# Attention products with 128 rows and 128 columns of the array, and two heads transposed at once

## The chip, the cores and the metric

The kernel runs on one core of a Trainium2 chip. Its time is the device time in microseconds (us) of one execution. Three runs of the kernel before gave 2948.76, 2953.93 and 2954.27 us; the median is 2953.93.

## The reference

The input is one sequence of 512 tokens with 1024 features. A first block of two layers, then a second block of one layer, all in float32:

```python
for l in range(2):
    x = layer_norm(ALPHA * x + 0.5 * swiglu(x, ...))          # ffn1
    x = layer_norm(ALPHA * x + token_mixer(x, ...))           # latent + sparse attention
    x = layer_norm(ALPHA * x + 0.5 * swiglu(x, ...))          # ffn2
# second block: gated linear attention, convolution, differential attention, then experts
x = x + mix @ w_out
x = x + hier_moe(rms_norm(x), ...)
```

The token mixer has two attentions of eight heads each. Latent attention (`mla_attention`) is causal, with 64 + 32 features per query and key, and 64 per value. Sparse attention (`nsa_attention`) has 64 features, two groups of four heads that share keys and values, and three branches whose results are added under a gate: attention over 31 compressed blocks of keys (`compress`: windows of 32 tokens through a small network with a Gelu), over selected blocks, and over a window. With 512 tokens all eight blocks are selected and the window covers everything, so these two are causal attentions with keys and values of their own. Differential attention in the second block has four heads; each takes two causal softmax maps of 64 features and subtracts the second, times a factor, from the first.

## The kernel before

Float32 values are split in two halves of TensorE's faster float32 type: `hi` is the rounded value (ScalarE), `lo` the rest (VectorE, `split`, L205 and L206). A product of two such values is three products, hi x hi, lo x hi and hi x lo (`mm3`, L223 to L225); only lo x lo is left out.

**A unit** (`Unit`) is one head and one branch. It goes through four stages: `prep` (transposes the head's queries and keys so that features lie on the partitions, and splits them), `scores` for four blocks of 128 queries (`prob_block`: score products L499, the causal mask as a product with an identity L500, maximum L502, exponential L503, reciprocal L504, scaling by GpSimd L105), `turn` (`prob_T`: transposes of the probabilities, L516, and their split) and `values` (`products`: L124 and L127). `attend` runs units as a pipeline: in one step, unit n makes its scores, unit n-1 its transposes, unit n-2 its values; the preparation of unit n+2 stands at the end of the step. A first-block layer has 8 latent units and then 16 sparse ones (8 heads x 2 branches). Between the stages 16 chunks of a gate projection are woven in (`gate_chunk`, L223 to L225 with tile `g`), at 0.62 of a part per point. The order within each engine's queue is then fixed by the scheduler of the language when the program is built: it keeps the program's priority, and moves an instruction up where one before it is not ready by its own model.

**Rows and columns of the array.** A product's rows are its contraction, its columns the width of its weights. Latent scores have 96 features, three products with 96 rows. Sparse and differential scores stack the query: `q2` holds the hi half in partitions 0 to 63 and the lo half in 64 to 127, `kk` the key's hi half twice. One product with 128 rows gives (q hi + q lo) x k hi, a second one with 64 rows q hi x k lo (`kl`). In the values the weights are v hi and v lo side by side (128 columns), so that a product with the probabilities' hi half writes v hi x p hi to the upper and v lo x p hi to the lower 64 partitions of the output; the second product has only the 64 columns of v hi, with the probabilities' lo half. `put` adds the two output halves at the end.

**Preparation.** `head_q` and `head_k` handle one head: four transposes of 128 tokens x 64 features (L836, L824), then ScalarE writes the hi half (L838, L841; for keys twice, L825 and L826) and VectorE the lo half (L839, L842, L827). Sparse keys are prepared when a group's first head begins (heads 0 and 4), for both branches; queries once per head. Differential attention calls both for each of the two maps of a head (L1342, L1343).

**The compressed branch.** When the second head of a pair is prepared, `compressed` computes the scores of both heads against 32 compressed keys: for four blocks of tokens and two heads a product with 128 rows (L912) and one with 64 (L913), each 32 wide; then mask, softmax and gate on VectorE and ScalarE, four transposes (L930), and a split into two tiles. `nsa_end` adds this branch to the head's output with two products that have 32 rows (L762, L763), against `vcb`, the compressed values that `compress` made beside the query projection.

**Banks.** Score products, key and query transposes and gate chunks share four PSUM banks (`pa`), the transposes of probabilities and the outputs four others (`pb`).

Of the kernel before, what the change touches and what calls it, by code (L numbers as in the profile page):

```python
# [87 lines left out]
class Unit:  # L88
# [31 lines left out]
    def products(self, j, out, start, stop):  # L120

        mm, v = self.b.nc.tensor.matmul, self.v(j)
        ph, pl = self.b.keys_T(j, self.pT)
        both = lambda: mm(out[:, j * 128:], v, ph, start=start and j == 0, stop=stop and j == NT - 1)  # L124
        if j == 0:
            both()
        mm(out[:64, j * 128:], v[:, :64], pl, start=False, stop=False)  # L127
        if j > 0:
            both()


class DiffUnit(Unit):
# [28 lines left out]
class Build:  # L161
# [381 lines left out]
    def mixer_(self, es, l):  # L543
# [10 lines left out]
        ksw = [p1.tile([128, NT, 2, 64], F32, name=f"k{b}") for b in "sw"]  # L554
        vsw = [p1.tile([128, NT, 2, 64], F32, name=f"v{b}") for b in "sw"]
        gn = p1.tile([128, NT, 24], F32, name="gn")
        vcb = p1.tile([64, 2, 2, 64], F32R, name="vcb")
        kcd = [[p1.tile([128, 32], F32R, name=f"kcd{g}{j}") for j in range(2)] for g in range(2)]
        pro = ExitStack()
        p2 = pro.enter_context(tc.tile_pool(name=f"p2{l}", bufs=1, reuse_waits="tile"))  # L560
# [166 lines left out]
        def nsa_begin():  # L727
            big = [pm.tile([128, 3072], F32R, name=f"big{j}", tag=("q96", "k96")[j]) for j in range(2)]
            st["on"] = [x[:, :2048].rearrange("p (c n) -> p c n", c=4) for x in big]
            st["vn"] = [x[:, 2048:].rearrange("p (t g k d) -> p t g k d", t=NT, g=2, k=2) for x in big]  # L730
            st["pc"] = [self.base.tile([128, 2, 512], F32R, name="pc", tag=t) for t in ("gB", "bB")]
            for br in range(2):
                self.split(st["vn"][br][:, :, :, 0], st["vn"][br][:, :, :, 1], vsw[br])

        def nsa_prep(h, br):
            g = h // 4

            def prep():
                if h == 0 and br == 0:
                    nsa_begin()  # L740
                if h % 4 == 0 and br == 0:
                    kk = self.wh.tile([128, 1024], F32R, name="kk", tag="hi").rearrange("p (k n) -> p k n", k=2)
                    kl = self.wl.tile([128, 1024], F32R, name="kl", tag="lo").rearrange("p (k n) -> p k n", k=2)
                    for b in range(2):
                        self.head_k(kk[:, b], kl[:, b], lambda t: ksw[b][:, t, g, :])
                    st["k", g] = kk, kl
                kk, kl = st["k", g]
                if br == 0:
                    st["q", h % 2] = self.head_q(qn, h)
                q2 = st["q", h % 2]  # L750
                if h % 2 == 1 and br == 0:
                    self.compressed(h - 1, st["q", 0], st["q", 1], kcd[g], gn, cmask, valid,
                                    [x[:64, (h // 2) % 2] for x in st["pc"]])
                return (q2, q2[:64]), (kk[:, br], kl[:64, br])
            return prep

        def nsa_end(h):
            g, r = h // 4, slice((h % 2) * 32, (h % 2) * 32 + 32)

            def end(po):  # L760
                pc = [x[r, (h // 2) % 2] for x in st["pc"]]
# [57 lines left out]
    def head_k(self, kk, kl, src):  # L819

        nc = self.nc
        ps = self.pa()
        for t in range(NT):
            nc.tensor.transpose(ps[:64, t * 128:t * 128 + 128], src(t), self.ident)  # L824
        nc.scalar.activation(kk[:64], ps[:64], AF.Copy)  # L825
        nc.scalar.activation(kk[64:], ps[:64], AF.Copy)  # L826
        nc.vector.tensor_tensor(kl[:64], ps[:64], kk[:64].bitcast(F32), ALU.subtract)  # L827

    def head_q(self, qn, h, q2=None, g=None):

        nc = self.nc
        if q2 is None:
            q2 = self.wh.tile([128, 1024], F32R, name="q2", tag="hi")[:, :T]
        ps = self.pa()
        for t in range(NT):
            nc.tensor.transpose(ps[:64, t * 128:t * 128 + 128], qn[:, t, h, :], self.ident)  # L836
        if g is None:
            nc.scalar.activation(q2[:64], ps[:64], AF.Copy)  # L838
            nc.vector.tensor_tensor(q2[64:], ps[:64], q2[:64].bitcast(F32), ALU.subtract)  # L839
        else:  # L840
            nc.scalar.activation(q2[:64], ps[:64], AF.Copy, scale=g)  # L841
            nc.vector.scalar_tensor_tensor(q2[64:], ps[:64], g, q2[:64].bitcast(F32), op0=ALU.mult, op1=ALU.subtract)  # L842
        return q2

    def windows(self, kc_tm, vc_tm, blks):

# [17 lines left out]
    def compress(self, l, p2, blks, kcd, vcb):  # L864

        nc, a, par = self.nc, self.a, self.par
        w2 = p2.tile([128, 2, 128], F32, name="w2")
        nc.scalar.dma_start(w2, a["cw2"][l])
        for j in range(2):
            for g in range(2):  # L870
                nc.gpsimd.memset(kcd[g][j].bitcast(F32), 0.0)  # L871
        for kv in range(2):
            blk = blks[:, 2 * kv:2 * kv + 2].rearrange("p c t -> p (c t)")[:, :992].rearrange(
                "p (m n) -> p m n", m=16)
            ph = self.pa()[:, :62]
            for m in range(16):
                if m % 8 == 0:
                    w1 = self.wr.tile([128, 1024], F32, name="w1", tag="raw").rearrange("p (c h) -> p c h", c=8)
                    nc.sync.dma_start(w1, a["cw1"][l, kv, m // 8])
                nc.tensor.matmul(ph, w1[:, m % 8, :], blk[:, m],  # L880
                                 start=m == 0, stop=m == 15)
                yield
            b1 = par[:, (P_B1K, P_B1V)[kv]:(P_B1K, P_B1V)[kv] + 1]
            if kv == 0:
                hid = self.tmp.tile([128, 512], F32, name="hid", tag="tmp")[:, :62]
                nc.scalar.activation(hid, ph, AF.Gelu_apprx_tanh, bias=b1)
                pk = self.pa()[:, :62]
                nc.tensor.matmul(pk, w2[:, 0, :], hid, start=True, stop=True)
                for g in range(2):
                    hi, lo = kcd[g][0][:, :31], kcd[g][1][:64, :31]  # L890
                    nc.scalar.activation(hi, pk[:, g * 31:g * 31 + 31], AF.Copy)
                    nc.vector.tensor_tensor(lo, pk[:64, g * 31:g * 31 + 31], hi[:64].bitcast(F32), ALU.subtract)
            else:
                hid = self.tmp.tile([128, 512], F32, name="hid", tag="tmp")[:, :128]
                h4 = hid.rearrange("p (g r c) -> p g r c", g=2, r=2)
                nc.vector.memset(hid, 0.0)
                for g in range(2):
                    nc.scalar.activation(h4[:, g, 0, :31], ph[:, g * 31:g * 31 + 31], AF.Gelu_apprx_tanh, bias=b1)
                    nc.vector.tensor_copy(h4[:, g, 1, :], h4[:, g, 0, :])
                    pv = self.pa()[:64, :64]  # L900
                    nc.tensor.matmul(pv, hid[:, g * 64:g * 64 + 64], w2[:, 1, :64], start=True, stop=True)
                    self.split(vcb[:, g, 0], vcb[:, g, 1], pv)

    def compressed(self, h, qe, qo, kcd, gn, cmask, valid, out):

# [405 lines left out]
    def diff_attention(self, es, dqk, dv, row, mT):  # L1311
# [25 lines left out]
        def prep(h):  # L1337
            q2, kk = (self.wh.tile([128, 1024], F32R, name=n, tag="hi").rearrange("p (m n) -> p m n", m=2)
                      for n in ("q2", "kk"))
            kl = self.wl.tile([128, 1024], F32R, name="kl", tag="lo").rearrange("p (m n) -> p m n", m=2)  # L1340
            for m in range(2):
                self.head_q(dqk[0], 2 * h + m, q2[:, m], qk[:64])  # L1342
                self.head_k(kk[:, m], kl[:, m], lambda t: dqk[1][:, t, 2 * h + m, :])  # L1343
# [3 lines left out]
            return [(q2[:, m], q2[:64, m]) for m in range(2)], [(kk[:, m], kl[:64, m]) for m in range(2)]  # L1347

        def end(h, po):
            o = self.tmp.tile([128, 512], F32, name="o", tag="tmp")  # L1350
# [598 lines left out]
```

## Time and profile before

| what | value |
|---|---|
| median of three runs | 2953.93 us |
| profiled execution | 2947.45 us, span 2945.7 us |
| TensorE products busy (share of span), instructions | 2831.6 us (96%), 14451 |
| VectorE busy | 1647.5 us (56%), 3229 |
| ScalarE busy | 1192.5 us (40%), 2174 |
| GpSimd busy | 349.0 us (12%), 386 |
| mean granted clock of TensorE | 0.974 |

One execution is profiled by the hardware. In the profile PE is TensorE's products, PEld its weight loads, DVE VectorE, ACT ScalarE, POOL GpSimd, SP the engine that starts most transfers. A duration of a product runs from its start to its modelled end; products overlap in the array, so the time that one takes of the engine is read from the distance between starts. PEclk is the granted clock of TensorE as a share of full speed; it has two levels, 0.50 (1.2 GHz) and 1.00 (2.4 GHz), and a mean over a stretch lies between.

Times in the rows are counted from the start of the span. In the first layer latent scores begin at 488.8 us and sparse scores at 560.6; in the second layer sparse attention begins near 1760; differential attention begins with its transposes at 2602.4.

### The profile page before, as it was taken

To read this page: it belongs to the slowest core of one execution; us is meant where nothing else is said; L and a number is where in the kernel's file an instruction comes from. 1 tells how busy PE (TensorE), PEld (TensorE's weight loads), DVE (VectorE), ACT (ScalarE), POOL (GpSimd) and SP (SyncE) were. 2 spreads that over 40 slices of the span, in tenths; PEclk is the share of its full clock that TensorE was granted. 3 is DMA by queue.
4 is the path that set the end of the run, shared out by engine and by line. 5 is a ranking of instruction groups with operands and counts; after the bars stand their busy time and mean duration, and the time that the engine had idled before them with its cause. 6 is when DMAs were issued, how large, how long until landed. Compare 5 with 4: busy or idle time off the path is not lost. (4 is left out here: it accounts for less than half of the span.)

```text
span 2945.7 us, 38251 instructions
## 1 busy us (share of the span) xinstructions
PE 2831.6 (96%) x14451; PEld 2294.7 (78%) x14451; DVE 1647.5 (56%) x3229; ACT 1192.5 (40%) x2174; POOL 349.0 (12%) x386
## 2 busy tenths in 40 slices
PE   8999999999999999999999999999999988789797
PEld 8888888777788888888888877778888876567575
DVE  4332376767554332543326687765433268876988
ACT  4222145655432321323213575553222133264675
POOL 0000001222000000000000022200000005432343
PEclk9999999999999999999999999999999999889899
DMA  4323232111622322223222311162232221104896
GB/s 159 100 94 100 89 98 90 55 44 58 207 94 93 114 94 94 93 93 115 93 93 91 104 55 43 47 215 93 93 115 93 94 71 48 48 16 158 297 369 256
DMA packets 95553, 322.19 MB, mean 109 GB/s; under 512 B 11120, under 2 KB 11904, under 8 KB 95360
## 3 DMA queue, kind: packets, MB, share of 16 engines
q1 hardware_dynamic: 85248, 285.91, 28.6%
q0 software_dynamic: 5184, 18.88, 1.8%
q10 hardware_dynamic: 4928, 14.88, 1.5%
q8 instruction: 116, 1.90, 0.3%
q14 instruction: 77, 0.63, 0.1%
HBM read 294.98 MB, written 24.64 MB: 109 GB/s over the span
## 5 line engine op out<-in xcount | busy, mean ns | idle before, releaser
L205 ACT ACTIVATE hi<-raw 128x1024 fp32r<-128x1024 f32 (+4 forms) x370 | 380.9, 1034 | 1112.9 <-PE pa L224 324.2
L206 DVE TENSOR_TENSOR lo<-raw,hi 128x1024 fp32r<-128x1024 f32 (+4 forms) x370 | 443.1, 1199 | 675.1 <-ACT hi L205 674.6
L223 PE MATMUL pa<-xh,hi 128*128 128x512 f32 (+1 forms) x808 | 302.2, 374 | 0.9 <-DVE xh L276 0.9
L224 PE MATMUL pa<-xl,hi 128*128 128x512 f32 (+1 forms) x808 | 301.7, 373 | 0.0
L225 PE MATMUL pa<-xh,lo 128*128 128x512 f32 (+1 forms) x808 | 301.0, 373 | 0.0
L223 PE MATMUL pb<-xh,hi 128*128 128x512 f32 (+1 forms) x784 | 289.9, 370 | 1.6 <-ACT hi L205 1.6
L225 PE MATMUL pb<-xh,lo 128*128 128x512 f32 (+1 forms) x784 | 289.8, 370 | 0.2 <-DVE lo L206 0.2
L224 PE MATMUL pb<-xl,hi 128*128 128x512 f32 (+1 forms) x784 | 289.8, 370 | 0.0
L424 DVE TENSOR_TENSOR sg<-sg,pb 128x512 f32<-128x512 f32 x88 | 60.5, 688 | 272.5 <-PE pb L225 270.4
L223 PEld LDWEIGHTS pa<-xh,hi 128*128 128x128 f32 x808 | 152.4, 189 | 29.3 <-DVE xh L276 1.7
L224 PEld LDWEIGHTS pa<-xl,hi 128*128 128x128 f32 x808 | 152.5, 189 | 26.6
L225 PEld LDWEIGHTS pa<-xh,lo 128*128 128x128 f32 x808 | 152.3, 188 | 26.5
L223 PEld LDWEIGHTS pb<-xh,hi 128*128 128x128 f32 x784 | 147.8, 188 | 26.7 <-ACT hi L205 1.8
L225 PEld LDWEIGHTS pb<-xh,lo 128*128 128x128 f32 x784 | 147.8, 189 | 25.5 <-DVE lo L206 0.4
L223 PE MATMUL pa<-hi,hh 128*128 128x512 f32 x416 | 165.9, 399 | 1.5 <-ACT hh L205 1.5
L224 PEld LDWEIGHTS pb<-xl,hi 128*128 128x128 f32 x784 | 147.6, 188 | 24.9
L224 PE MATMUL pa<-lo,hh 128*128 128x512 f32 x416 | 164.8, 396 | 0.1
L225 PE MATMUL pa<-hi,hl 128*128 128x512 f32 x416 | 164.5, 395 | 0.0
L223 PE MATMUL pa<-hi,xh 128*128 128x512 f32 (+4 forms) x416 | 155.9, 377 | 2.7 <-DVE xh L276 1.5
L224 PE MATMUL pa<-lo,xh 128*128 128x512 f32 (+4 forms) x416 | 151.1, 364 | 6.4 <-DVE lo L206 6.3
L225 PE MATMUL pa<-hi,xl 128*128 128x512 f32 (+4 forms) x416 | 149.3, 361 | 0.0
L871 POOL MEMSET kcd<- 128x32 f32 x8 | 0.6, 163 | 1217.8 <-PE pb L225 1217.8
(550 smaller groups left out, 6154.3 us busy)
## 6 DMA issues: line engine op xcount, KB each, us to landing
raw<-in_gu SPq DMA_DIRECT2D x176, 512.0 KB, 3.3
raw<-in_wd SPq DMA_DIRECT2D x88, 512.0 KB, 3.3
mraw<-in_eg SPq DMA_DIRECT2D x51, 512.0 KB, 7.2
raw<-in_win_g SPq DMA_DIRECT2D x32, 512.0 KB, 3.3
mraw<-in_ed SPq DMA_DIRECT2D x20, 512.0 KB, 7.5
sig<-sg SPq DMA_DIRECT2D x32, 256.0 KB, 2.0
raw<-in_wp SPq DMA_DIRECT2D x16, 512.0 KB, 5.1
sg<-sig SPq DMA_DIRECT2D x32, 256.0 KB, 4.0
```

Of the source, the lines that this page charges most:

```text
L205: first = nc.scalar.activation(hi, src, AF.Copy)
L206: last = (eng or nc.vector).tensor_tensor(lo, src, hi.bitcast(F32), ALU.subtract)
L223: nc.tensor.matmul(out, sh, mh, start=start, stop=False)
L224: nc.tensor.matmul(out, sh, ml, start=False, stop=False)
L225: nc.tensor.matmul(out, sl, mh, start=False, stop=stop)
L424: nc.vector.tensor_tensor(sg, sg, pu, ALU.mult)
L871: nc.gpsimd.memset(kcd[g][j].bitcast(F32), 0.0)
```

## The change

The lo products of the scores and values, the compressed scores and the compressed branch's last product get all 128 rows and 128 columns, and two heads are transposed together.

- `Unit.products`: the lo product has the weights v hi and v lo too (128 columns), and follows the hi product in every block.
- Scores: `kl` holds the key's lo half twice, and both products have 128 rows. So q lo x k lo is added too.
- `pair_cols` transposes two heads at once (128 tokens x 128 features, four transposes). `heads_q` writes head 0 as hi over lo, head 1 as lo over hi. `heads_k` writes, for each of the two, the hi half twice (two copies on ScalarE) and the lo half twice (two subtractions on VectorE).
- Sparse keys are prepared for both groups, both branches, in the preparation of the first sparse unit; queries and the compressed scores with the first head of a pair instead of the second.
- The compressed probabilities lie in one tile (hi in partitions 0 to 63, lo in 64 to 127), and `vcb` has a version of 128 rows and 128 columns for either head of a pair, with zeros in the other head's rows. `compress` makes it with two products and two splits per group instead of one. `nsa_end` has one product instead of two.
- Differential attention prepares its two maps with one `heads_q` and one `heads_k`.

```diff
 def products(self, j, out, start, stop):
-        both = lambda: mm(out[:, j * 128:], v, ph, start=start and j == 0, stop=stop and j == NT - 1)
-        if j == 0:
-            both()
-        mm(out[:64, j * 128:], v[:, :64], pl, start=False, stop=False)
-        if j > 0:
-            both()
+        mm(out[:, j * 128:], v, ph, start=start and j == 0, stop=False)
+        mm(out[:, j * 128:], v, pl, start=False, stop=stop and j == NT - 1)
...
-        vcb = p1.tile([64, 2, 2, 64], F32R, name="vcb")
+        vcb = p1.tile([128, 2, 2, 128], F32R, name="vcb")
...
-                return (q2, q2[:64]), (kk[:, br], kl[:64, br])
+                if h % 2 == 0 and br == 0:
+                    q2 = self.wh.tile([128, 1024], F32R, name="q2", tag="hi").rearrange("p (k n) -> p k n", k=2)
+                    st["q"] = [q2[:, x] for x in range(2)]
+                    self.heads_q(st["q"], lambda t: qn[:, t, h:h + 2, :].rearrange("p h d -> p (h d)"))
+                    self.compressed(h, *st["q"], kcd[g], gn, cmask, valid,
+                                    [st["pc"][k * 64:k * 64 + 64, (h // 2) % 2] for k in range(2)])
+                q2 = st["q"][h % 2]
+                return (q2, q2), (kk[:, br], kl[:, br])
...
-                nc.tensor.matmul(po[:64], vcb[r, g, 0], pc[1], start=False, stop=False)
-                nc.tensor.matmul(po, vcb[r, g].rearrange("p k d -> p (k d)"), pc[0], start=False, stop=True)
+                nc.tensor.matmul(po, vcb[:, g, h % 2], st["pc"][:, (h // 2) % 2], start=False, stop=True)
...
+    def heads_k(self, out, src):
+        ps = self.pair_cols(src)
+        for x, (kk, kl) in enumerate(out):
+            own = slice(x * 64, x * 64 + 64)
+            both = slice(0, 64), slice(64, 128)
+            for r in both:
+                nc.scalar.activation(kk[r], ps[own], AF.Copy)
+            for r in both:
+                nc.vector.tensor_tensor(kl[r], ps[own], kk[own].bitcast(F32), ALU.subtract)
...
+    def heads_q(self, out, src, g=None):
+        ps = self.pair_cols(src)
+        for x, q2 in enumerate(out):
+            own, other = (slice(y * 64, y * 64 + 64) for y in (x, 1 - x))
+            if g is None:
+                nc.scalar.activation(q2[own], ps[own], AF.Copy)
+                nc.vector.tensor_tensor(q2[other], ps[own], q2[own].bitcast(F32), ALU.subtract)
...
-                nc.tensor.matmul(ps[:, c], q2[:64, s], kcd[1][:64], start=False, stop=True)
+                nc.tensor.matmul(ps[:, c], q2[:, s], kcd[1], start=False, stop=True)
```

## Rows read from the trace of the kernel before

**Rows 1.** Page, part 1: busy us (share of the span) x instructions.
```profile
PE 2831.6 (96%) x14451; PEld 2294.7 (78%) x14451; DVE 1647.5 (56%) x3229; ACT 1192.5 (40%) x2174; POOL 349.0 (12%) x386
```

**Rows 2.** Table of stretches: busy us of each engine, clock, DMA share, GB/s.
```profile
488.80:560.60 71.80, 69.72 (x427) 56.46 (x427) 58.99 (x145) 54.30 (x144) 22.48 (x31) 1.00 0.15 52
560.60:740.00 179.40, 178.36 (x883) 128.75 (x882) 125.82 (x316) 103.56 (x279) 40.87 (x65) 0.93 0.16 54
1760.00:1938.00 178.00, 176.81 (x880) 128.52 (x879) 123.31 (x304) 100.95 (x268) 39.06 (x62) 0.95 0.20 68
2602.40:2695.00 92.60, 83.33 (x377) 57.25 (x377) 67.54 (x192) 58.30 (x137) 38.66 (x53) 0.83 0.19 61
```

**Rows 3.** TensorE's longest wait, 560 to 740: total us, times, longest us.
```profile
PE pa L912 <- DVE q L839: 0.4, 1, 0.4
```

**Rows 4.** Timeline of TensorE, sparse attention: start us, us, instruction, count.
```profile
642.68 0.39 PE L516 MATMUL pb<-ident,pr 128*128 128x128 f32 x2
642.83 0.42 PE L127 MATMUL pb<-pT,big 128*64 128x384 f32 x1
643.08 0.34 PE L124 MATMUL pb<-pT,big 128*128 128x384 f32 x1
643.26 0.34 PE L499 MATMUL pa<-kk,q 128*128 128x384 f32 x1
643.53 0.44 PE L499 MATMUL pa<-kl,q 64*128 64x384 f32 x1
643.90 0.23 PE L500 MATMUL pa<-maskb,identb 128*128 128x128 bf16 x1
...
645.94 0.39 PE L499 MATMUL pa<-kk,q 128*128 128x512 f32 x1
646.26 0.49 PE L499 MATMUL pa<-kl,q 64*128 64x512 f32 x1
646.68 0.23 PE L500 MATMUL pa<-maskb,identb 128*128 128x128 bf16 x1
...
647.25 0.28 PE L124 MATMUL pb<-pT,big 128*128 128x128 f32 x1
647.46 0.45 PE L762 MATMUL pb<-pc,vcb 32*64 32x512 f32 x1
647.75 0.39 PE L763 MATMUL pb<-pc,vcb 32*128 32x512 f32 x1
648.06 0.33 PE L499 MATMUL pa<-kk,q 128*128 128x128 f32 x1
```

**Rows 5.** Timeline of TensorE, latent attention.
```profile
545.09 0.39 PE L225 MATMUL pa<-xh,g 128*128 128x512 f32 x1
545.32 0.34 PE L499 MATMUL pa<-th 96*128 96x384 f32 x1
...
545.85 0.23 PE L500 MATMUL pa<-maskb,identb 128*128 128x128 bf16 x1
...
553.30 0.27 PE L499 MATMUL pa<-tl,th 96*128 96x128 f32 x1
553.41 0.28 PE L499 MATMUL pa<-th,tl 96*128 96x128 f32 x1
```

**Rows 6.** Timeline of TensorE, end of the first pair's compressed scores.
```profile
574.26 0.28 PE L912 MATMUL pa<-kcd,q 128*128 128x32 f32 x1
574.47 0.33 PE L913 MATMUL pa<-kcd,q 64*128 64x32 f32 x1
574.73 0.58 PE L499 MATMUL pa<-kk,q 128*128 128x256 f32 x1
```

**Rows 7.** Table of stretches: the first of eight falls of the clock.
```profile
574.60:581.40 6.80, 6.80 (x17) 4.08 (x18) 3.24 (x10) 1.96 (x6) 0.69 (x2) 0.50 0.00 0
```

**Rows 8.** Groups by line and shape: VectorE's key splits, busy us, mean ns.
```profile
L827 DVE TENSOR_TENSOR kl<-pa,kk 64x512 fp32r<-64x512 f32 x16 | 10.9, 681 | 3.6 <-ACT kk L826 3.5
```

**Rows 9.** TensorE's longest wait on score tiles, 2595 to 2695.
```profile
PE pa L499 <- DVE q L842: 2.0, 1, 2.0
```

More of the change, by code (lines that the diff above doesn't have):

```diff
@@ L730, in nsa_begin @@
             st["vn"] = [x[:, 2048:].rearrange("p (t g k d) -> p t g k d", t=NT, g=2, k=2) for x in big]
-            st["pc"] = [self.base.tile([128, 2, 512], F32R, name="pc", tag=t) for t in ("gB", "bB")]
+            st["pc"] = self.base.tile([128, 2, 512], F32R, name="pc", tag="gB")
             for br in range(2):
@@ L740, in prep @@
                     nsa_begin()
-                if h % 4 == 0 and br == 0:
-                    kk = self.wh.tile([128, 1024], F32R, name="kk", tag="hi").rearrange("p (k n) -> p k n", k=2)
-                    kl = self.wl.tile([128, 1024], F32R, name="kl", tag="lo").rearrange("p (k n) -> p k n", k=2)
+                    for x in range(2):
+                        st["k", x] = [p.tile([128, 1024], F32R, name=n, tag=tag).rearrange("p (k n) -> p k n", k=2)
+                                      for p, n, tag in ((self.wh, "kk", "hi"), (self.wl, "kl", "lo"))]
@@ L744, in prep @@
                     for b in range(2):
-                        self.head_k(kk[:, b], kl[:, b], lambda t: ksw[b][:, t, g, :])
-                    st["k", g] = kk, kl
+                        self.heads_k([[z[:, b] for z in st["k", x]] for x in range(2)],
+                                     lambda t: ksw[b][:, t].rearrange("p g d -> p (g d)"))
                 kk, kl = st["k", g]
-                if br == 0:
-                    st["q", h % 2] = self.head_q(qn, h)
-                q2 = st["q", h % 2]
@@ L751, in prep @@
-                if h % 2 == 1 and br == 0:
-                    self.compressed(h - 1, st["q", 0], st["q", 1], kcd[g], gn, cmask, valid,
-                                    [x[:64, (h // 2) % 2] for x in st["pc"]])
-                return (q2, q2[:64]), (kk[:, br], kl[:64, br])
+                if h % 2 == 0 and br == 0:
[4 more added lines that the diff above has]
+                                    [st["pc"][k * 64:k * 64 + 64, (h // 2) % 2] for k in range(2)])
@@ L755, in nsa_prep @@
+                q2 = st["q"][h % 2]
+                return (q2, q2), (kk[:, br], kl[:, br])
             return prep
         def nsa_end(h):
-            g, r = h // 4, slice((h % 2) * 32, (h % 2) * 32 + 32)
+            g = h // 4
             def end(po):
-                pc = [x[r, (h // 2) % 2] for x in st["pc"]]
-                nc.tensor.matmul(po[:64], vcb[r, g, 0], pc[1], start=False, stop=False)
-                nc.tensor.matmul(po, vcb[r, g].rearrange("p k d -> p (k d)"), pc[0], start=False, stop=True)
+                nc.tensor.matmul(po, vcb[:, g, h % 2], st["pc"][:, (h // 2) % 2], start=False, stop=True)
@@ L817, in mixer_, with pair_cols @@
         self.down_ln(ND, yT, a["wo"][l], l, 1, 1.0, 4)
-    def head_k(self, kk, kl, src):
-        nc = self.nc
+    def pair_cols(self, src):
         ps = self.pa()
         for t in range(NT):
[L824 to L829, printed above, removed]
-        nc = self.nc
[L832 to L843, printed above, removed]
+            self.nc.tensor.transpose(ps[:, t * 128:t * 128 + 128], src(t), self.ident)
+        return ps
@@ new lines, in heads_k @@
+    def heads_k(self, out, src):
+        nc = self.nc
+        ps = self.pair_cols(src)
[7 more added lines that the diff above has]
+    def heads_q(self, out, src, g=None):
+        nc = self.nc
+        ps = self.pair_cols(src)
[4 more added lines that the diff above has]
+                nc.vector.tensor_tensor(q2[other], ps[own], q2[own].bitcast(F32), ALU.subtract)
+            else:
+                nc.scalar.activation(q2[own], ps[own], AF.Copy, scale=g[own])
+                nc.vector.scalar_tensor_tensor(q2[other], ps[own], g[own], q2[own].bitcast(F32),
+                                               op0=ALU.mult, op1=ALU.subtract)
@@ L889, in compress @@
                 for g in range(2):
-                    hi, lo = kcd[g][0][:, :31], kcd[g][1][:64, :31]
-                    nc.scalar.activation(hi, pk[:, g * 31:g * 31 + 31], AF.Copy)
-                    nc.vector.tensor_tensor(lo, pk[:64, g * 31:g * 31 + 31], hi[:64].bitcast(F32), ALU.subtract)
-            else:
-                hid = self.tmp.tile([128, 512], F32, name="hid", tag="tmp")[:, :128]
-                h4 = hid.rearrange("p (g r c) -> p g r c", g=2, r=2)
+                    self.split(kcd[g][0][:, :31], kcd[g][1][:, :31], pk[:, g * 31:g * 31 + 31])
+            else:
+                hid = self.tmp.tile([128, 512], F32, name="hid", tag="tmp")
+                h5 = hid.rearrange("p (g e k r c) -> p g e k r c", g=2, e=2, k=2, r=2)
                 nc.vector.memset(hid, 0.0)
                 for g in range(2):
[L898 to L902, printed above, removed]
+                    nc.scalar.activation(h5[:, g, 0, 0, 0, :31], ph[:, g * 31:g * 31 + 31], AF.Gelu_apprx_tanh, bias=b1)
+                    nc.vector.tensor_copy(h5[:, g, 0, 1, 0, :], h5[:, g, 0, 0, 0, :])
+                    nc.vector.tensor_copy(h5[:, g, 1, :, 1, :], h5[:, g, 0, :, 0, :])
+                    for e in range(2):
+                        pv = self.pa()[:, :64]
+                        nc.tensor.matmul(pv, h5[:, g, e].rearrange("p k r c -> p (k r c)"), w2[:, 1, :64],
+                                         start=True, stop=True)
+                        self.split(vcb[:, g, e, :64], vcb[:, g, e, 64:], pv)
     def compressed(self, h, qe, qo, kcd, gn, cmask, valid, out):
@@ L1340, in prep @@
             kl = self.wl.tile([128, 1024], F32R, name="kl", tag="lo").rearrange("p (m n) -> p m n", m=2)
-            for m in range(2):
-                self.head_q(dqk[0], 2 * h + m, q2[:, m], qk[:64])
-                self.head_k(kk[:, m], kl[:, m], lambda t: dqk[1][:, t, 2 * h + m, :])
+            two = lambda w: lambda t: dqk[w][:, t, 2 * h:2 * h + 2, :].rearrange("p m d -> p (m d)")
+            self.heads_q([q2[:, m] for m in range(2)], two(0), qk)
+            self.heads_k([(kk[:, m], kl[:, m]) for m in range(2)], two(1))
             if h == 0:
@@ L1346, in prep @@
                     self.split(vd[0][:, :, t, :], vd[1][:, :, t, :], dv[:, t])
-            return [(q2[:, m], q2[:64, m]) for m in range(2)], [(kk[:, m], kl[:64, m]) for m in range(2)]
+            return [(q2[:, m], q2[:, m]) for m in range(2)], [(kk[:, m], kl[:, m]) for m in range(2)]
         def end(h, po):
```

## The prediction

> **What bounds the kernel now.** I read the engine table of the page first: TensorE is busy for 96% of the span [rows 1], so the question is what each changed instruction takes of TensorE's queue, stage by stage. The second view was the table of stretches [rows 2]: latent attention of the first layer (488.8 to 560.6), the sparse-attention part of both layers (560.6 to 740 and 1760 to 1938) and the differential attention of the second block (2602.4 to 2695). The reader is to see that TensorE is busy for 178.4 of 179.4 us in the sparse part, VectorE for 125.8 (70%), ScalarE for 103.6 (58%), and that the granted clock is below 1 there (0.93 and 0.95, 0.83 in the differential part) while it is 1.00 in latent attention. Third, the table of waits: in the whole sparse part of the first layer TensorE's longest wait is 0.4 us [rows 3]. So it is issue-bound, and what counts is the distance from one start to the next, not the duration in a row (durations overlap). That distance comes from the timeline, the fourth view [rows 4, 5].
>
> **The change part by part.**
>
> *Scores (prob_block, L499).* A block is the query's two halves, hi over lo, against the key's hi half twice (128 rows, `kk,q`), then the query's hi half against the key's lo half (64 rows, `kl,q`), then the mask. In [rows 4] the 384-wide block runs from 643.26 to the mask at 643.90, 0.64 us, and the 512-wide one from 645.94 to 646.68, 0.74. Latent attention has three 96-row products of 384 between 545.32 and 545.85, 0.177 each, and a 512-wide product takes 0.23 (545.09 to 545.32) [rows 5]. Two without a change of rows would take 0.35 and 0.46: the 64-row product costs 0.28 to 0.29 us more per block, about 0.09 before it and 0.19 after it, whatever the width. The changed kernel gives it 128 rows; I take 0.28 per block. Blocks: 2 layers x 16 units x 4 = 128, and 4 heads x 2 maps x 4 = 32 in the differential part. That is 35.8 us and 9.0 us. Bounds: none of it, to all of it.
>
> The row shows this price only where rows change between 128 and 64. The Trainium skill ("TensorE: Matmul & The Clock Gate", Why this matters for your kernels) says that a single small-K matmul takes the same time as one with K=128, so that filling up the rows would return nothing; another page ("TensorEngine Tiling (Array Packing)", Key Properties) says that changing the tiling mode drains the engine. The trace agrees with the second, with 0.28 us for the way there and back. By the first alone the score term would be zero; it is a rival below.
>
> *Compressed scores (L912, L913).* 64 pairs (2 layers x 4 head pairs x 8) of 32-wide products alternate between 128 and 64 rows, 0.21 us apart [rows 6], 0.42 a pair. The nearest narrow row without the change is the 128-wide product of latent attention, 0.11 (553.30 to 553.41) [rows 5]. So 0.20 x 64 = 12.8 us. Bounds: 0 to 12.8, as 0.11 is the load of 128 columns, which stays.
>
> *End of a head (L762, L763).* From L124 at 647.25 over two 32-row products to the next at 648.06 are 0.81 us [rows 4]. Afterwards one 128-row product of 512: 0.11 + 0.23 = 0.34. 0.47 x 16 heads = 7.5 us (0.23 x 16 = 3.7 if the rows cost nothing).
>
> *Transposes.* Two heads at once halve them: keys 16 to 8 and queries 32 to 16 per layer, 64 to 32 in the differential part, so 48 + 32 fewer. One takes 0.11 us (642.68 to 643.26 are 0.58; less two 384-wide products of 0.177, 0.23 for two) [rows 4]: 5.3 us and 3.5 us.
>
> *Values (L124, L127).* The lo product goes from 64 to 128 columns. The same 0.58 us leaves no room for a change of column width, so nothing is gained. The narrow last block loses: with 128 columns of weights a 128-wide product takes 0.11 [rows 5], with 64 it could go at a quarter of 0.23. 0.055 x 48 units = -2.6 us.
>
> The Trainium skill counts 128x64 as a tiling mode of its own ("TensorEngine Tiling (Array Packing)", Tiling Modes); by that, each of the seven alternations of a unit would also return something like the row change, and the sum would be some 30 us larger. The 0.58 us above disagrees, and I leave it out.
>
> *Compressed values (compress, v part).* Two more small products and two more splits per layer beside the projection's products; no row shows them. I take -1 us for both layers (0 to -4, if the chain behind the Gelu lies open).
>
> So 35.8 + 12.8 + 7.5 + 5.3 - 2.6 - 1 = 57.8 us for the two mixers.
>
> *Clock.* A clock of 0.93 over 179.4 us and 0.95 over 178, with the level at 1.2 GHz in the falls [rows 7], means some 25 + 18 = 43 us at half clock [rows 2]. There are eight falls, one per head pair; the first begins at 574.6, right after the sixteen 32-wide products of the first pair, which run by turns to 574.73 [rows 6, 7]. Those will take 16 x 0.11 = 1.8 us and not 3.4, so I expect most falls to go. Worth at most half of 43, 21 us (all falls gone, everything TensorE-paced); nothing if they stay. I take 15.
>
> *VectorE as cover.* heads_k writes kl to both halves: 4 more subtractions of 0.68 us per layer and 8 in the differential part [rows 8], 2.7 and 5.4 us. TensorE has hidden VectorE so far. Now the sparse stretch would be 179.4 - 36.4 = 143 us with 125.8 + 2.7 = 128.5 us of VectorE, 90%. The highest share under a busy TensorE is in latent attention, 59.0 of 71.8, 82% [rows 2]. At 82% the stretch would be 157 us, at 90% 143; I take 86%, 149, a toll of 6.5 us per layer, -13. It includes the first preparation: both groups' keys are split at once there (8 ScalarE copies, 8 VectorE subtractions, two score banks held meanwhile) and the compressed scores move up two units, behind them on VectorE; TensorE's queue behind the first narrow product waits for them. If it lies open it costs up to ten of these subtractions, 0 to 7 us per layer. No DMA is added or moved, and GpSimd and SP have the same work.
>
> *Differential part.* 9.0 + 3.5 = 12.5 us fewer on TensorE, but it is idle 9 of 92.6 us, among them 2.0 waiting for a query split [rows 2, 9], VectorE gets 5.4 more, and the clock is low for some 31 us. Bounds: -5.4 (all of the added VectorE work open) to +27 (12.5 and half of 31). I take +5, near the idle engine's row: what TensorE saves there it mostly waits.
>
> **Sum.** 57.8 + 15 - 13 + 5 = 65 us. The profiled execution took 2947.45 us (span 2945.7), which gives 2882; the median of the runs is 2953.93, 6.5 above it, and 65 less is **2889 us**, my forecast.
>
> **The rivals.**
>
> *VectorE sets the pace of the sparse part.* Then it does not go beyond the 82% that latent attention shows: 128.5/0.82 = 157 and 126/0.82 = 154 us, a gain of 23 + 24 = 47, nothing in the differential part: 2907. For it: 90% is higher than any stretch of before under a busy TensorE. Against it: at 82% TensorE was still busy 97%, so 82% is no ceiling. Chance 0.20.
>
> *All lands.* No toll, all eight falls gone and most of those in the differential part: 57.8 + 20 + 17 = 95, 2859. For it: the units have a whole step between scores and their use. Against: the 90%, and a differential part whose low clock comes with an idle TensorE. Chance 0.15.
>
> *Rows cost nothing.* If the 0.28 us hangs on something other than the row count (the half-height weights' place, the order of the products), scores and compressed scores return nothing: 3.7 + 8.8 - 3.6 = 9 us, 2945; the change would then not do what it says. Against it: three 96-row products in the same loop, with the same mask, show none of it. Chance 0.05. This is the first of the skill's rules above.
>
> *Slower.* The loop score - maximum - exponential - reciprocal - scaling, not TensorE, already sets the unit's length, and VectorE can't be used more than the present 70%, 69% and 73%: 128.5/0.70 = 183.6, 126/0.69 = 182.6, and 5.4/0.73 = 7.4 more in the differential part, together +16: 2970. It decides if VectorE's share in the sparse part stays at 70% after the change. Against it: latent attention runs the same loop at 82%, and TensorE's waits in the sparse part are 0.4 us at most. Chance 0.05.
>
> **How the numbers follow.** The forecast has 0.55, with its own range of 2873 to 2905. The range reaches to the all-lands case on one side and past the VectorE case on the other: 2855 to 2925, which leaves out the two last rivals and the tails. A measurement of this kernel tells about 0.2%, 6 us, from no change. Only the slower case is above that, with a bit of it within: slower 0.04, same 0.02, faster 0.94.
>
> **What would show it.** In the changed profile the two products of a 384-wide block start 0.18 us apart, and the mask 0.18 after the second; the sixteen 32-wide products run 0.11 apart; the clock of the sparse stretches is 0.98 or above; these stretches last about 149 us with VectorE at 86%, and TensorE has waits for VectorE there of some 5 us that it has not now. The prediction is wrong if the block still takes 0.64, if falls of the clock come at the old places, or if TensorE's new waits in the sparse part exceed 15 us per layer.

## The result, and the profile after

The changed kernel takes 2905.49 us (median of four runs, 2904.68 to 2908.53) against 2951.52 of the kernel before in the same comparison: a ratio of 0.9846, 95% interval 0.9829 to 0.9863. It is faster by 46 us. The forecast was 65 us; 2905.49 lies half a us outside the range given to the forecast itself (2873 to 2905) and inside the whole range (2855 to 2925).

The page of the changed kernel, parts 1 and 2 (columns as in [rows 1], and the clock in 40 slices):

```profile
PE 2767.0 (95%) x14363; PEld 2281.6 (78%) x14363; DVE 1652.7 (57%) x3253; ACT 1191.8 (41%) x2178; POOL 347.5 (12%) x386
...
PEclk9999999899999999999999999999999998879899
```

TensorE is 65 us less busy, and the span of this execution is 39 us shorter (2906.7 against 2945.7). So TensorE did get rid of the work; part of what it got rid of came back as idle time. Nor did the clock gain as a whole: its mean is 0.972 after 0.974. Where the idle time came, the table of stretches tells. I cut each layer's attention where the first head's first product with `vcb` starts: the *front* is latent attention with the preparation of the sparse part and its first scores, the *rest* runs to the same product of the last head. Before, as in [rows 2] with other borders (front, rest, front, rest, differential part):

```profile
488.90:602.60 113.70, 110.93 (x629) 86.04 (x629) 88.53 (x221) 77.49 (x208) 32.87 (x47) 0.97 0.14 50
602.60:743.80 141.20, 140.90 (x699) 101.95 (x698) 98.21 (x243) 81.33 (x215) 30.48 (x49) 0.94 0.19 65
1681.10:1794.70 113.60, 110.83 (x628) 86.25 (x628) 88.57 (x221) 77.42 (x208) 32.85 (x47) 0.97 0.14 50
1794.70:1933.60 138.90, 138.45 (x699) 100.41 (x698) 96.92 (x241) 81.20 (x215) 30.74 (x49) 0.96 0.19 66
2602.40:2688.90 86.50, 77.23 (x347) 52.34 (x346) 64.19 (x179) 55.06 (x133) 38.66 (x53) 0.82 0.16 53
```

After:

```profile
489.10:605.30 116.20, 109.78 (x632) 89.09 (x631) 92.54 (x227) 80.08 (x211) 31.86 (x46) 0.93 0.16 53
605.30:719.80 114.50, 112.60 (x668) 91.10 (x667) 90.53 (x239) 77.34 (x213) 32.71 (x51) 1.00 0.23 79
1660.60:1776.50 115.90, 108.86 (x630) 88.15 (x631) 92.73 (x227) 79.77 (x210) 31.83 (x46) 0.94 0.16 53
1776.50:1891.20 114.70, 112.79 (x668) 91.08 (x667) 91.30 (x239) 77.42 (x213) 32.47 (x51) 1.00 0.23 80
...
2560.60:2647.00 86.40, 65.47 (x310) 48.62 (x310) 70.70 (x186) 55.91 (x133) 37.23 (x53) 0.80 0.16 53
```

The reader is to see three things. The rests are 26.7 and 24.2 us shorter, at a clock of 1.00 instead of 0.94 and 0.96, with VectorE at 79 and 80%. The fronts are some 2.4 us *longer*, at 0.93 and 0.94 instead of 0.97. And the differential part has not moved, though TensorE is busy there for 65.5 us instead of 77.2; VectorE has gone from 64.2 to 70.7. Fronts and rests together are 46 us shorter, the two spans only 39: the other parts of these two executions differ by 7 us the other way, which is what they lie off the medians (2947.45 us is 4 below the one, 2908.53 is 3 above the other).

The prediction put the border at the first sparse score. By that border, latent attention and sparse attention of the first layer, then of the second, after the change:

```profile
489.10:567.80 78.70, 72.88 (x425) 59.63 (x425) 62.90 (x149) 55.42 (x144) 20.99 (x30) 0.93 0.14 48
567.80:719.80 152.00, 149.50 (x874) 120.57 (x873) 120.17 (x316) 102.00 (x281) 43.58 (x67) 0.98 0.22 75
1660.60:1739.20 78.60, 72.22 (x424) 58.98 (x425) 63.10 (x149) 55.12 (x142) 20.94 (x30) 0.95 0.14 48
1739.20:1891.20 152.00, 149.43 (x874) 120.25 (x873) 120.93 (x316) 102.06 (x282) 43.36 (x67) 0.98 0.22 76
```

And before, without the first layer's latent attention (71.8 us in [rows 2]):

```profile
560.60:744.10 183.50, 182.46 (x902) 131.85 (x901) 128.15 (x319) 104.61 (x280) 40.87 (x65) 0.93 0.18 61
1681.10:1752.90 71.80, 69.77 (x427) 56.41 (x427) 59.01 (x145) 54.22 (x143) 22.46 (x31) 1.00 0.15 52
1752.90:1933.90 181.00, 179.81 (x902) 130.49 (x901) 126.67 (x318) 104.47 (x280) 41.13 (x65) 0.95 0.18 62
```

The sparse part is 31.5 and 29.0 us shorter; latent attention is 7 us longer in each layer. The first sparse preparation stands there, and with it the stop shown below and the first pair's narrow products, which had stood behind the border before.

The products themselves are as forecast. Timeline of TensorE in the changed kernel (columns as in [rows 4]):

```profile
636.40 0.26 PE L916 MATMUL pa<-kcd,q 128*128 128x32 f32 x1
636.51 0.26 PE L917 MATMUL pa<-kcd,q 128*128 128x32 f32 x1
636.62 0.37 PE L495 MATMUL pa<-kk,q 128*128 128x256 f32 x1
...
636.99 0.42 PE L495 MATMUL pa<-kk,q 128*128 128x384 f32 x1
637.24 0.33 PE L495 MATMUL pa<-kl,q 128*128 128x384 f32 x1
637.42 0.23 PE L496 MATMUL pa<-maskb,identb 128*128 128x128 bf16 x1
...
639.83 0.28 PE L125 MATMUL pb<-pT,big 128*128 128x128 f32 x1
639.94 0.45 PE L758 MATMUL pb<-pc,vcb 128*128 128x512 f32 x1
640.22 0.22 PE L495 MATMUL pa<-kk,q 128*128 128x128 f32 x1
```

The second product of a 384-wide block takes 0.18 us to the mask (0.37 in [rows 4]); the block's 0.43 in all still holds 0.07 of the mask product that went before it. Narrow products run 0.11 apart (0.21 in [rows 6]); the end of a head takes 0.39 from L125 (0.81 from L124 in [rows 4]).

What went wrong in the front is in the same view, here with VectorE above and TensorE below, first layer (the last line of TensorE is the same place in the second):

```profile
552.68 4.22 DVE L831 TENSOR_TENSOR kl<-pa,kk 64x512 fp32r<-64x512 f32 x6
557.18 1.40 DVE L831 TENSOR_TENSOR kl<-pa,kk 64x512 fp32r<-64x512 f32 x2 [0.28 <-ACT kk L829]
558.61 0.69 DVE L841 TENSOR_TENSOR q<-pa,q 64x512 fp32r<-64x512 f32 x1
```

```profile
554.89 0.40 PE L221 MATMUL pa<-xh,g 128*128 128x512 f32 x1
559.44 0.37 PE L916 MATMUL pa<-kcd,q 128*128 128x32 f32 x1 [4.15 <-DVE q L841]
559.65 0.37 PE L917 MATMUL pa<-kcd,q 128*128 128x32 f32 x1
...
1730.86 0.26 PE L916 MATMUL pa<-kcd,q 128*128 128x32 f32 x1 [4.15 <-DVE q L841]
```

```profile
557.50:574.60 17.10, 14.41 (x53) 11.91 (x54) 9.47 (x27) 4.82 (x17) 2.96 (x5) 0.50 0.01 2
1731.70:1745.40 13.70, 12.35 (x45) 10.00 (x46) 6.62 (x22) 3.82 (x13) 2.59 (x4) 0.50 0.00 1
```

All eight key subtractions of both groups stand ahead of the query's split on VectorE. TensorE's queue has the first compressed product next, which needs that split, and stops for 4.15 us. In the first layer the clock falls to its lower level inside that stop (557.5) and stays there for 17.1 us; in the second, which has the same stop, it falls at 1731.7, 0.8 us after the stop's end, for 13.7 us: the last two rows, stretches as in [rows 7]. The eight falls of before are gone from their old places; in these parts two long ones have come in their stead.

### The profile page after: what moved, and what is told of

Read it like the earlier page. It is cut to its first block, busy times and chain, and to the rows that moved or that the text cites. A ratio compares the mean times of both kernels' runs of the same rounds, so it can differ in the third digit from the quotient of the medians.

```text
span 2906.7 us, 38055 instructions
## 1 busy us (share of the span) xinstructions
PE 2767.0 (95%) x14363; PEld 2281.6 (78%) x14363; DVE 1652.7 (57%) x3253; ACT 1191.8 (41%) x2178; POOL 347.5 (12%) x386
```

## The experiments

Every kernel was timed against the kernel before; ratios are to it. For the changed kernel the ratio is 0.9846 (0.9829 to 0.9863).

| run | edit | median us | ratio (95%) |
|---|---|---|---|
| e1_rows64 | sparse scores, 64 rows again | 2937.62 | 0.9951 (0.9935 to 0.9968) |
| e2_cols64 | values, 64 columns again | 2908.43 | 0.9854 (0.9837 to 0.9870) |
| e3_group_keys | keys paired by group | 2906.24 | 0.9842 (0.9826 to 0.9859) |
| e4_cmp_late | compressed scores a unit later | 2890.22 | 0.9790 (0.9773 to 0.9806) |
| e5_both | e3 and e4 | 2885.21 | 0.9774 (0.9758 to 0.9791) |
| e6_zero_half | zeros instead of the second subtraction | 2894.31 | 0.9802 (0.9785 to 0.9818) |
| e7_diff_before | differential part as before | 2905.83 | 0.9837 (0.9821 to 0.9853) |
| e8_cmp_rows | kernel before, compressed scores with 128 rows | 2925.08 | 0.9906 (0.9889 to 0.9922) |
| e9_late_zero | e4 and e6 | 2880.79 | 0.9749 (0.9719 to 0.9778) |
| e10_all_three | e3, e4 and e6 | 2880.06 | 0.9753 (0.9725 to 0.9781) |

Fronts, rests and the differential part (first query transpose to the start of the last value product), worked out from the starts in each profile, us:

| kernel | front 1, 2 | rest 1, 2 | differential |
|---|---|---|---|
| before | 113.7, 113.6 | 141.2, 138.9 | 86.5 |
| changed | 116.2, 115.9 | 114.5, 114.7 | 86.8 |
| e3 | 113.8, 112.4 | 117.1, 117.1 | 85.8 |
| e4 | 108.7, 108.4 | 114.3, 113.9 | 86.8 |
| e5 | 104.0, 104.0 | 115.4, 115.4 | 87.9 |
| e6 | 113.9, 114.5 | 114.5, 114.5 | 81.7 |
| e9 | 106.7, 105.3 | 114.0, 113.9 | 81.7 |
| e10 | 103.3, 103.2 | 115.4, 115.3 | 81.6 |

### Do the rows cost, or something else? (e1)

```diff
-                return (q2, q2), (kk[:, br], kl[:, br])
+                own = slice(h % 2 * 64, h % 2 * 64 + 64)
+                return (q2, q2[own]), (kk[:, br], kl[own, br])
```

> The changed kernel, with the second score product of the sparse units back at 64 rows (32 units, 128 blocks); everything else stays. Theory (the change of rows costs 0.28 us per block): 36 us back, 2941 against 2905; the 384-wide block takes 0.64 us again. Rival (rows cost nothing, the old price hung on the order or place of the products): 2905 +- 4.

2937.62 us, 32 more than the changed kernel, 0.25 per block. A 384-wide block in its profile:

```profile
645.08 0.42 PE L495 MATMUL pa<-kk,q 128*128 128x384 f32 x1
645.43 0.44 PE L495 MATMUL pa<-kl,q 64*128 64x384 f32 x1
645.80 0.23 PE L496 MATMUL pa<-maskb,identb 128*128 128x128 bf16 x1
```

0.37 from the 64-row product to the mask again. Order, places and preparation are those of the changed kernel, so it is the number of rows that costs. The rival is refuted. That the price hangs on the change of rows and not on each product of 64 rows is not shown by e1, as its 64-row products never follow one another; [rows 4] speak for it, where two 32-row products in a row lose 0.24 us together (0.81 against 0.11 + 2 x 0.23).

Not all of the 32 us is the blocks' own price. The sparse part of e1 has three falls of the clock that the changed kernel has not (3.4, 10.2 and 3.4 us); the longest, with the clock last but two:

```profile
1787.20:1797.40 10.20, 10.20 (x28) 6.75 (x29) 5.44 (x17) 4.01 (x11) 2.02 (x3) 0.50 0.22 77
```

At half speed the three are worth up to 8.5 us. Between starts at full clock the price of a block is the 0.28 of the forecast, 36 us for the 128 blocks; so not all of it comes out in the time.

### Do the columns cost? (e2)

```diff
-        mm(out[:, j * 128:], v, ph, start=start and j == 0, stop=False)
-        mm(out[:, j * 128:], v, pl, start=False, stop=stop and j == NT - 1)
+        both = lambda: mm(out[:, j * 128:], v, ph, start=start and j == 0, stop=stop and j == NT - 1)
+        if j == 0:
+            both()
+        mm(out[:64, j * 128:], v[:, :64], pl, start=False, stop=False)
+        if j > 0:
+            both()
```

> The changed kernel, with the values' lo product back at 64 columns and in the old order. Theory (a change of columns costs nothing, the narrow last block is 0.055 us shorter for each of 48 units): 2902 to 2905, at most 3 us faster. Rival (a change of columns drains the array as one of rows does): some 30 us slower, 2935.

2908.43 us, 3 more than the changed kernel, and the intervals of the two ratios overlap: no difference that can be told. By the starts in its profile the width of the weights changes 360 times between 64 and 128 columns in these attentions; at the price of the rows, 0.28 us there and back, that would be some 50 us (the expectation had some 30). So the columns show no price like that of the rows. My 2.6 us for the narrow last block are not seen either.

### Where the gain of the fronts went (e3, e4, e5)

```diff
 # e3: transpose both branches of one group together, at heads 0 and 4
-        ksw = [p1.tile([128, NT, 2, 64], F32, name=f"k{b}") for b in "sw"]
+        ksb = p1.tile([128, NT, 2, 2, 64], F32, name="ksb")
+        ksw = [ksb[:, :, :, b] for b in range(2)]
...
+                if h % 4 == 0 and br == 0:
+                    st["k", g] = [...]
+                    self.heads_k([[z[:, b] for z in st["k", g]] for b in range(2)],
+                                 lambda t: ksb[:, t, g].rearrange("p b d -> p (b d)"))
...
 # e4: the compressed scores with the pair's first window unit
+                if h % 2 == 0 and br == 1:
                     self.compressed(h, *st["q"], kcd[g], gn, cmask, valid, ...)
```

> The changed kernel, with the pairs of sparse keys taken by group (both branches of one group transposed together) instead of by branch, so that only half of the key copies and subtractions stand in the first sparse preparation and the other half in that of head 4, as in the kernel before; the same instructions in all. Theory (the burst of eight 0.68 us subtractions before the query split makes TensorE wait 4 us per layer, and the low clock behind it, 17 and 14 us at half speed, follows from that): the wait shrinks to under 1 us, the falls go, 15 to 20 us faster, about 2888. Rival (the narrow compressed products at that place pull the clock down by themselves): 4 to 8 us faster, the falls stay.

2906.24 us: no gain, a miss of my theory. The wait itself did go, from 4.2 to 0.3 us; TensorE now waits 1.3 us at another place. Waits of TensorE between 548 and 577 us in e3 (columns as in [rows 3]):

```profile
PE pa L495 <- DVE kl L831: 1.3, 1, 1.3
PE pa L219 <- ACT pr L499: 0.4, 1, 0.4
PE pa L916 <- DVE q L841: 0.3, 1, 0.3
```

But the clock still fell to half in both fronts (13.7 and 10.2 us). In the first layer fourteen of the sixteen narrow products ran in that fall; in the second they had run 0.11 apart at full clock, and the fall began 0.6 us after the last of them had started. The fronts got 2.4 and 3.5 us shorter and the rests, with the other half of the keys at head 4, 2.6 and 2.4 longer. So the burst is moved, not saved, and the length of the stop alone does not explain the low clock.

> The changed kernel, with the compressed scores made in the preparation of a pair's first window unit, one unit later; keys and queries are prepared as in the changed kernel. Theory (TensorE waits because the compressed products need the query split at the end of the burst, and its queue stands still behind them): the wait goes, as the next user of the split comes a unit later, 12 to 20 us faster, about 2890. Rival (the burst holds the score banks, so TensorE waits wherever the products stand): within 4 us of 2905.

2890.22 us, 15 less than the changed kernel, all of it in the fronts (7.5 us each). There is no wait for the query split any more; the narrow products stand a unit later, 0.11 apart at full clock. One fall of 6.8 us stays in each front. In both layers it comes after the narrow products (0.6 to 1.5 us after the last one's start), and two waits for key subtractions (1.3 and 0.5 us) stand before them. Timeline of TensorE in e4, first layer:

```profile
557.41 0.30 PE L495 MATMUL pa<-th 96*128 96x128 f32 x1 [1.27 <-DVE kl L832]
559.23 0.35 PE L495 MATMUL pa<-th 96*128 96x256 f32 x1 [0.48 <-DVE kl L832]
...
564.03 0.26 PE L917 MATMUL pa<-kcd,q 128*128 128x32 f32 x1
564.14 0.26 PE L918 MATMUL pa<-kcd,q 128*128 128x32 f32 x1
```

Waits and clock account for the 7.5 us, within 1 us. In the first layer the waits for VectorE's splits went from 4.5 to 1.8 us and the time at the lower level from 17.1 to 6.8, which is 5.1 us at half speed: 7.8. In the second they went from 5.1 to 1.8 and from 13.7 to 6.8: 6.7. So what cost was the narrow products at the head of TensorE's queue, behind VectorE's burst, and the low clock that came with the stop; how much of the low clock is due to the stop and how much to the products is not shown.

> Both edits of the two runs before together: keys paired by group, and the compressed scores one unit later. With keys by group the front of the sparse part was 2.4 us shorter per layer and the part from the first to the last head's end 2.5 us longer, with the compressed scores later the front was 7.6 us shorter and nothing was longer. Theory (the second burst, at head 4, costs what the first one gives back): 2890 +- 4. Rival (the second burst costs only because the narrow products stand right behind it): 2880 +- 4.

2885.21 us. The fronts are 104.0 us with no fall in them; the rests are 1.1 and 1.5 us longer than in e4. The median lies between the two ranges, 0.8 us below the theory's and 1.2 above the rival's: the second burst costs less than in e3 once no narrow products follow it, but it does cost, so neither is borne out as it stood. Stretches of e5, with the clock (last but two):

```profile
557.00:575.00 18.00, 17.55 (x109) 14.20 (x109) 15.96 (x46) 12.30 (x35) 6.15 (x10) 1.00 0.12 46
575.00:593.00 18.00, 18.00 (x113) 14.93 (x112) 16.07 (x41) 14.42 (x40) 5.66 (x8) 1.00 0.26 89
```

VectorE is at 89% in both, and TensorE at 98 and 100%: over these 36 us the 82% of latent attention was no ceiling.

### VectorE's added subtractions, and the differential part (e6, e7)

```diff
 # e6: kl has zeros below; q2 has the hi half on top for both heads (in heads_q, left out here)
+            nc.gpsimd.memset(kl[64:].bitcast(F32), 0.0)
...
-            for r in both:
-                nc.vector.tensor_tensor(kl[r], ps[own], kk[own].bitcast(F32), ALU.subtract)
+            nc.vector.tensor_tensor(kl[:64], ps[own], kk[own].bitcast(F32), ALU.subtract)
...
```

> The changed kernel, with the lower half of kl set to zero by GpSimd instead of a second subtraction on VectorE, and the query's hi half always on top (so q lo x k lo is left out, as in the kernel before): 4 subtractions fewer per sparse layer and 8 fewer in the differential part, all products still with 128 rows. Theory (VectorE's burst of splits is what TensorE waits for in front of the sparse part and in the differential part): the front gets 3 to 5 us shorter per layer and the differential part up to 5 us, 2892 to 2898. Rival (the burst that counts is ScalarE's copies and the order, or TensorE waits for GpSimd instead): 2903 or more.

2894.31 us, 11 less and in the theory's range. The differential part went from 86.8 to 81.7; the fronts got 2.3 and 1.4 us shorter, less than the 3 to 5 expected. Key subtractions on VectorE in the differential part, in the changed kernel and in e6 (columns as in [rows 8]):

```profile
L831 DVE TENSOR_TENSOR kl<-pa,kk 64x512 fp32r<-64x512 f32 x16 | 11.0, 688 | 0.8 <-ACT kk L829 0.5
```

```profile
L830 DVE TENSOR_TENSOR kl<-pa,kk 64x512 fp32r<-64x512 f32 x8 | 5.5, 684 | 1.2 <-ACT kk L829 1.0
```

5.5 us less of VectorE, 5.1 us less of time: in this part the saved subtractions come back almost whole.

> The changed kernel, with the differential attention's preparation and scores as in the kernel before (one head at a time, 64 rows). Theory (the 12.5 us that TensorE saves there are spent waiting for VectorE and ScalarE, and the part lasts 86.8 us against 86.5): 2905 +- 4. Rival (the part did gain and lost elsewhere by accident of one profile): 2912 to 2918.

```diff
...
+            for m in range(2):
+                self.head_q(dqk[0], 2 * h + m, q2[:, m], qk[:64])
+                self.head_k(kk[:, m], kl[:, m], lambda t: dqk[1][:, t, 2 * h + m, :])
...
+            return [(q2[:, m], q2[:64, m]) for m in range(2)], [(kk[:, m], kl[:64, m]) for m in range(2)]
```

2905.83 us, and the part lasts 86.5 us: the differential edit is worth nothing that can be told. TensorE's waits in this part come to 20.4 us in the changed kernel and 8.9 in the kernel before, 11.5 more, as much as it is less busy (77.2 to 65.5). The four longest after the change:

```profile
PE pa L495 <- DVE q L844: 6.6, 3, 3.5
PE pa L495 <- ACT ring L499: 5.2, 4, 2.8
PE pa L495 <- DVE kl L831: 3.2, 2, 3.0
PE pb L512 <- POOL ring L145: 2.3, 2, 2.1
```

The first was 2.0 us before [rows 9].

### What the narrow products do to the clock (e8)

```diff
 # the key's lo half is written to all 128 partitions
-                    hi, lo = kcd[g][0][:, :31], kcd[g][1][:64, :31]
...
+                    self.split(kcd[g][0][:, :31], kcd[g][1][:, :31], pk[:, g * 31:g * 31 + 31])
...
-                nc.tensor.matmul(ps[:, c], q2[:64, s], kcd[1][:64], start=False, stop=True)
+                nc.tensor.matmul(ps[:, c], q2[:, s], kcd[1], start=False, stop=True)
```

> The kernel before, with one part of the change alone: the lo product of the compressed scores has 128 rows (64 products). Theory (the change of rows costs 0.20 us per pair, and the eight falls of the clock in the sparse parts come from the 3.4 us of narrow products by turns): 13 us for the rows and 15 for the falls, 2924 against 2952. Rival (the falls come from the sparse scores' pattern as a whole): the falls stay, 13 us, 2939.

2925.08 us, 28 less than the kernel before, as the theory had it. In its sparse stretches the clock is back to 0.99, against 0.93 and 0.95 in [rows 2]; of the eight falls two of 3.4 us are left, behind the first pair of each layer. The 64-row scores are still there, so they do not bring the other six by themselves. What of the narrow products brought them, their changes of rows or the time that they took, is not told apart. Stretches of e8, from the same places as in [rows 2]:

```profile
560.60:740.00 179.40, 177.70 (x944) 129.73 (x943) 133.35 (x327) 111.02 (x291) 41.12 (x65) 0.99 0.24 83
1746.60:1911.60 165.00, 163.90 (x877) 119.76 (x876) 122.24 (x303) 99.94 (x267) 38.65 (x61) 0.99 0.21 72
```

### Together (e9, e10)

> The changed kernel with two of the edits: compressed scores one unit later, and kl's lower half zero by GpSimd instead of a second subtraction. Theory (the first saves 15 us in the sparse fronts, the second 10 us, of which 5 in the differential part, and only the fronts' shares overlap): 2880 to 2885. Rival (with the narrow products gone from the front, VectorE's burst there is hidden anyway, so the second edit adds its 5 us in the differential part alone): 2885 to 2887.

> All three edits: keys by group, compressed scores later, kl's lower half zero by GpSimd. Theory (the fronts are clear of falls already with the first two, 2885; the third adds what it gave the differential part, 5 us): 2880 +- 3. Rival (the fronts still lose to the splits, so the third edit adds there too): 2875 or less.

2880.79 and 2880.06 us, 71 and 72 us faster than the kernel before and 25 faster than the change as it was made; both lie in their theory's range, and the two can't be told apart. In e10 the third edit takes 5 us off e5, as the theory said, and 6.3 off its differential part; e9 shows that keys by group can be left out.

## Why the prediction was right or wrong

The direction and the mechanism of the gain were right: changes of rows cost, changes of columns show no price, and the sparse stretches pay for it. The sum was 19 us too high. 14 of these lie in the toll taken for VectorE, 5 in the differential part.

- *Scores:* 0.28 per block forecast, 0.25 in e1 (32 us over 128 blocks), of which up to 8.5 us can be clock.
- *Compressed scores and clock:* 12.8 + 15 forecast, 28 us in e8. The places of the falls and what stands in front of them were read rightly from the timeline of before. In the changed kernel the clock of the sparse part is 0.98, as forecast; more than half of what low clock is left lies ahead of it, in latent attention.
- *End of a head:* 0.34 forecast, 0.39 measured. *Transposes* and *compressed values* were not tried alone; no run shows the 1 us taken for the latter.
- *Values:* the 2.6 us loss was not seen. The Trainium skill ("TensorEngine Tiling (Array Packing)", Tiling Modes and Key Properties) lists 64x128 and 128x64 as modes and says that a change of mode drains the engine. A price of the change shows for the rows (e1) and none for the columns (e2).
- *VectorE as cover:* this is the term that was mis-sized, and its reason was wrong. I took a toll of 6.5 us per layer and spread it over the sparse part, with VectorE at 86% as its pace. There is no such pace: the rests run at 79% with TensorE at 98%, and e5 shows 89% beside a full TensorE. Without the toll the two mixers were to gain 72.8 us (57.8 + 15). Fronts and rests, 507.4 us before, gained 46.1 (461.3), so the toll, with whatever else is off in the 72.8, is 27 us and not 13. With the edits of e10 they take 437.2, a gain of 70.2: 24 of the 27 come back, 12.9 and 12.7 of it in the fronts, while the rests get 0.9 and 0.6 longer. So the toll lay in the first preparation, which I had bounded at 7 us per layer: that bound counted the subtractions and left out that the clock falls at the stop and stays low behind it. e4, which moves only the compressed scores, gives 15 us back.
- That the sparse part, by the prediction's own border, is 31.5 and 29.0 us shorter where 30 each were forecast is in part luck: VectorE is at 79% in it and not at 86, and the first pair's narrow products have left it. The loss stands ahead of the border, 7 us per layer in latent attention, for which the prediction had no change.
- The rival in which VectorE sets the pace, whose 2907 us is closest to the time measured, has the right time by another cause: VectorE stays under its 82% in the rests with TensorE full, and goes past it in e5.
- *Differential part:* +5 forecast, nothing measured (e7). The bounds held it, my choice between them did not: the added subtractions took much of what TensorE gave (e6: 5.1 us).

65 less 14 for the toll and 5 for the differential part are the 46 measured.

What stays open: what starts the falls in the fronts, and why the first lasts 17.1 us and the second 13.7. That the narrow products prolong them would fit e4 and the first layer of e3, not its second, where the fall came behind them; no kernel kept the stop and left the products out.

## What to carry to other kernels

Products that alternate between 64 and 128 rows paid for it here, 0.28 us there and back, so padding the contraction to the full array, by a copy or by zeros, can be worth more than the work that it adds; alternating between 64 and 128 columns showed no price. Before work is gathered into one preparation, look at which instruction of the critical engine stands right behind it in the queue: here a stop of four microseconds, with the low clock behind it, cost 7.5 us that moving that instruction gave back (e4). In a part where the critical engine already waits, count the added work of the engine that it waits for, not the work saved.

## What the runs showed of the hardware

Not expected was that the clock falls where TensorE never waits for more than 0.4 us ([rows 3] for the first layer; the second shows the same). In the kernel before, a fall stands behind, in one place within, each of the eight groups of sixteen 32-wide products, most of which run in a row 0.21 us apart. With the same products 0.11 apart, six of the eight places have none (e8). And where GpSimd set the lower half of an operand to zero (e6), no wait of TensorE in the fronts is put down to GpSimd; leaving the same half to VectorE cost 5 us in the differential part, though there the waits for GpSimd's scaling rose a little in e6, from 2.3 to 3.6 us.
